# Turning the gated output of six head groups by a transposing transfer instead of TensorE transposes

## The chip, the cores and the metric

One core of one Trainium2 chip runs the whole program once. The metric is the device time of that run in microseconds (us); the median of three runs is what counts. Five engines work side by side, each on its own queue, in the order in which that queue was written: TensorE (PE) for products, VectorE (DVE), ScalarE (ACT) and GpSimd (POOL) for element work, and SyncE (SP), which here only starts transfers between memory and SBUF.

## The reference

The program is one decoder layer on 256 tokens of width 2048. A state-space part (SSD, 32 heads in 8 groups of 4) and an attention part (16 heads) read the same normalised input; their outputs, 2048 columns each, go together through `w_out`, and an MLP of width 8192 follows. What the change touches is the end of the SSD part:

```python
proj = jnp.einsum('bsd,de->bse', u, w_in)
z, xbc, dt_raw, q, k, v = jnp.split(proj, IN_SPLITS, axis=-1)
xbc = jax.nn.silu(causal_depthwise_conv(xbc, conv_w, conv_b))
...
y = ssd_chunked(xh, dt, a, bm, cm)
y = y + d_skip...[:, :, None] * xh
yg = y.reshape(b_, s_, SSM_GROUPS, -1) * jax.nn.silu(z.astype(f32)).reshape(b_, s_, SSM_GROUPS, -1)
yg = yg * lax.rsqrt(jnp.mean(yg * yg, axis=-1, keepdims=True) + EPS)
y_ssm = (yg.reshape(b_, s_, D_SSM) * ssm_norm_w.astype(f32)).astype(u.dtype)
...
return jnp.einsum('bse,ed->bsd', jnp.concatenate([y_ssm, y_att], axis=-1), w_out)
```

For each of the 8 groups the gated output `yg` is a block of 256 tokens by 256 columns in 32-bit numbers. It is computed with tokens on the partitions; the last product needs it with its columns on the partitions, so every block is turned (transposed) once.

## The kernel before, in words

**Products.** All large products run as three products of split numbers: ACT copies a 32-bit tile to a rounded `hi` (L150), DVE subtracts to get the rest `lo` (L151), and PE multiplies with both. Weights come in tiles of 256 rows by 512 columns (`raw`, four buffers, loaded by SP at L164, or by L159 and L160 where half of the tile was stored earlier). `hi` and `lo` have five buffers, so ACT and DVE can be at most five weight tiles ahead of PE. `gemm_features` gives columns on the partitions (16 products a tile, L540 and L543); `row_tile` gives tokens on the partitions (12 products, L382 to L384). Some tiles go through a scheme that saves one product in eight (`seven`, L469 to L471); it needs sums of weight tiles (L275, on DVE) and sums of the input (L428 to L431, on DVE, then split by L150 and L151), which go to buffers `tp`, `ah` and `al`.

**Order in time.** Up to 400 us the program computes B, C, a block of x, a unit for z and a second block of x, and then the same again for the other four groups (the second unit for z lies at 232 to 274 us); behind that come the blocks for q and k of the attention, and at 358 us a unit with token rows whose first `seven` is at 369 us. All that time PE works on these products; the SSD groups are side work in between.

**A group.** `ssd_group` is a generator that `pump` resumes: after each weight tile one waiting piece of work gets one turn. One group g loads its decay table `bc` (L859, ACT's queue; a tile of 128 x 1024 words, two buffers), makes `bn`, `xs`, `xdt` and others (L865 to L879), makes decay factors in place in `bc` (L895 and L896 on ACT, L897 on DVE, each for two chunks of 128 tokens), multiplies (PE L913, 8 small products that read `bc` and `xdt` and write a PSUM tile `ps`), adds and gates (DVE L916, L918), forms the sum of squares (ACT L922), its root (DVE L144, POOL L145) and scales (DVE L926, the last to write `yg`). Then PE turns `yg` by four transposes (L932) into a PSUM tile, and `split` writes it to `sh` and `sl` with the norm's weight (ACT L152, DVE L153). The PSUM tiles named `ps` (`psmall`) have two buffers.

**What sets the order.** The code gives the order in which work is offered; a scheduler then puts each instruction on its engine's queue by its own estimate of when it will be ready and by priorities. So an added wait can move instructions of other work on every queue. After the last group `drain` finishes the side work, the pool of the SSD tiles is closed (`ssd.close`), and its space goes to the buffers `ah`, `al`, `tp` of the next unit: their first loads and sums cannot start before the last reader of the SSD tiles is done.

Of the kernel before, what the change touches and what calls it, by code (L numbers as in the profile page):

```python
# [13 lines left out]
U16 = mybir.dt.uint16  # L14
AF = mybir.ActivationFunctionType
ALU = mybir.AluOpType

P = 128
S = 256
D = 2048  # L20
NT = S // P
# [23 lines left out]
AHEAD = 1_000_000  # L45
# [9 lines left out]
V_SEVENS = (1, 3, 5, 6)  # L55
QK_SEVENS = (1, 3, 5, 6)
PAIRS_AHEAD = 4
TURNS = ((1, 2, 4, 5), (3, 4, 8, 9))
LANDS = ((0, 3, 4, 6), (0, 6, 7, 10, 11))

# [20 lines left out]
def hymba_layer(ctx: ExitStack, tc: tile.TileContext, x, norm_mix_pre, w_in, conv_w, conv_b, dt_bias, a_log,  # L81
                d_skip, ssm_norm_w, w_out, norm_mix_post, norm_mlp_pre, w_up, w_down, norm_mlp_post,
                consts, out):
    nc = tc.nc
# [27 lines left out]
    sh = big.tile([P, NK, S], F32R, name="sh")  # L112
    sl = big.tile([P, NK, S], F32R, name="sl")
# [11 lines left out]
    ident = cp.tile([P, P], F32, name="ident")  # L125
# [12 lines left out]
    def psmall():  # L138
        return psm.tile([P, NB], F32, name="ps")
# [7 lines left out]
    def split(hi, lo, src, scale=None):  # L147

        if scale is None:
            return (nc.scalar.activation(hi, src, AF.Copy),  # L150
                    nc.vector.tensor_tensor(lo, src, hi.bitcast(F32), op=ALU.subtract))  # L151
        return (nc.scalar.activation(hi, src, AF.Copy, scale=scale),  # L152
                nc.vector.scalar_tensor_tensor(lo, src, scale, hi.bitcast(F32), op0=ALU.mult, op1=ALU.subtract))  # L153
# [104 lines left out]
    line, newest = {}, {}  # L258
# [34 lines left out]
    def next_pair():  # L293

        if not pairs:
            return
        src, (ca, c), k = pairs.pop(0)
        cb = slice(c, c + NB)
        d = places[len(paired) % len(places)]
        if len(paired) < len(places):  # L300
            nc.gpsimd.dma_start(d[:, 0:1], room["pairs"])
        nc.gpsimd.dma_start(d, src[k * KB * P:(k * KB + 1) * P, cb])
        nc.gpsimd.dma_start(d, src[(k * KB + 1) * P:(k * KB + 2) * P, cb], accum_op=ALU.add)
        paired.append((src, ca, k, d))

    paired = []
    places = [dram.tile([P, NB], F32, name=f"pair{i}") for i in range(PAIRS_AHEAD + 1)]

# [25 lines left out]

    waiting = deque()

    def pump(n=1):
        for _ in range(n):
            if waiting:
                work = waiting.popleft()  # L340
                if next(work, work) is not work:
                    waiting.append(work)

    def drain():
        while waiting:
            pump()
# [3 lines left out]
    def pump_beside(exact=False):  # L350

        if not beside:
            return
        work = beside.popleft()
        room["exact"] = exact
        with tc.issue_after(newest["act"].ins):
            next(work)
        flying.append(work)
# [143 lines left out]
    def unit(src, n, order, last, acc, more, combine, lag=0, at_end=(None, None), first=True, ending=None,  # L502
# [5 lines left out]
        for i, (k, by_seven) in enumerate(order):  # L508
            if i in TURNS[len(order) > 7]:
                pump_beside(len(order) > 7)  # L510
# [67 lines left out]
    w_pre, w_mlp, w_ssm, cb = par[:, 0:16], par[:, 16:32], par[:, 32:48], par[:, 48:80]  # L578
# [6 lines left out]
    rows = xp.tile([64, P], F32, name="rows")  # L585
# [132 lines left out]
    def steps():  # L718
# [5 lines left out]
        with tc.high_priority(offset=AHEAD):  # L724
            for _ in range(PAIRS_AHEAD):
                next_pair()
# [128 lines left out]
    def ssd_group(sp, g, bT, cT, xT, z):  # L855

        hs = slice(HPG * g, HPG * (g + 1))
        bc = sp.tile([P, HPG, S], F32, name="bc")
        nc.scalar.dma_start(bc, acs_d[hs].partition_broadcast(P))  # L859
        yield  # L860

        p = psmall()
        for c in range(NT):
            cs = slice(c * P, (c + 1) * P)
            nc.tensor.matmul(p[:, cs], bT[:, cs], cT[:, cs], start=True, stop=True)  # L865
        nc.tensor.transpose(p[:, S:S + P], bT[:, 0:P], ident)
        cbm = sp.tile([P, NT, P], F32, name="cbm")
        nc.vector.tensor_tensor(cbm, p[:, :S].rearrange("p (c i) -> p c i", c=NT),
                                triu[:, None, :].to_broadcast([P, NT, P]), op=ALU.mult)
        bn = sp.tile([P, P], F32, name="bn")  # L870
        nc.scalar.activation(bn, p[:, S:S + P], AF.Copy)

        p = psmall().rearrange("p (c f) -> p c f", c=NT)
        for c in range(NT):
            for f in range(2):
                nc.tensor.transpose(p[:, c, f * P:(f + 1) * P], xT[:, f, c * P:(c + 1) * P], ident)
        xs = sp.tile([P, NT, HPG, HD], F32, name="xs")
        nc.scalar.activation(xs.rearrange("p c r d -> p c (r d)"), p, AF.Copy)
        xdt = sp.tile([P, NT, HPG, HD], F32, name="xdt")  # L879
        for c in range(NT):  # L880
            nc.vector.tensor_tensor(xdt[:, c], xs[:, c], dt[:, c, hs, None].to_broadcast([P, HPG, HD]), op=ALU.mult)
        xdd = sp.tile([P, HPG, HD], F32, name="xdd")
        nc.gpsimd.tensor_tensor(xdd, xdt[:, 0], toend[:, hs, None].to_broadcast([P, HPG, HD]), op=ALU.mult)
        for c in range(NT):
            nc.gpsimd.tensor_tensor(xs[:, c], xs[:, c], skip_b[:, hs, None].to_broadcast([P, HPG, HD]), op=ALU.mult)
        yield

        for c in range(NT):
            m = bc[:, :, c * P:(c + 1) * P]
            for r in range(HPG):  # L890
                h = HPG * g + r
                if g in (2, 3):
                    nc.vector.tensor_scalar(m[:, r], m[:, r], acs[:, c, h:h + 1], 0.0, op0=ALU.subtract, op1=ALU.min)
                else:
                    nc.scalar.activation(m[:, r], m[:, r], AF.Relu, scale=-1.0, bias=acs[:, c, h:h + 1])  # L895
            nc.scalar.activation(m, m, AF.Exp, scale=1.0 if g in (2, 3) else -1.0)  # L896
            nc.vector.tensor_tensor(m, m, cbm[:, c, None, :].to_broadcast([P, HPG, P]), op=ALU.mult)  # L897

        p = psmall()
        nc.tensor.matmul(p[:, :S], bn, xdd.rearrange("p r d -> p (r d)"), start=True, stop=True)  # L900
        st = sp.tile([P, HPG * HD], F32, name="st")
        nc.scalar.activation(st, p[:, :S], AF.Copy)
        yield
        nc.tensor.matmul(p[:, S:], cT[:, P:], st, start=True, stop=True)
        yo = sp.tile([P, HPG, HD], F32, name="yo")
        nc.vector.tensor_tensor(yo, p[:, S:].rearrange("p (r d) -> p r d", r=HPG),
                                eacs[:, hs, None].to_broadcast([P, HPG, HD]), op=ALU.mult)
        nc.gpsimd.tensor_tensor(xs[:, 1], xs[:, 1], yo, op=ALU.add)
        yield
        p = psmall().rearrange("p (c r d) -> p c r d", c=NT, r=HPG)  # L910
        for c in range(NT):
            for r in range(HPG):
                nc.tensor.matmul(p[:, c, r], bc[:, r, c * P:(c + 1) * P], xdt[:, c, r], start=True, stop=True)  # L913

        yg = sp.tile([P, NT, HPG * HD], F32, name="yg")
        nc.vector.tensor_tensor(yg, p.rearrange("p c r d -> p c (r d)"), xs.rearrange("p c r d -> p c (r d)"),  # L916
                                op=ALU.add)
        nc.vector.tensor_tensor(yg, yg, z, op=ALU.mult)  # L918
        gs = sp.tile([P, NT], F32, name="gs")
        for c in range(NT):  # L920
            junk = sp.tile([P, HPG * HD], BF16, name="gj")
            nc.scalar.activation(junk, yg[:, c], AF.Square, accum_out=gs[:, c:c + 1])  # L922
        gr = sp.tile([P, NT], F32, name="gr")
        rsqrt_mean(gr, gs, HPG * HD)
        for c in range(NT):
            nc.vector.tensor_scalar(yg[:, c], yg[:, c], gr[:, c:c + 1], None, op0=ALU.mult)  # L926
        yield
        yield
        p = psmall().rearrange("p (f s) -> p f s", f=2)
        for f in range(2):  # L930
            for c in range(NT):
                nc.tensor.transpose(p[:, f, c * P:(c + 1) * P], yg[:, c, f * P:(f + 1) * P], ident)  # L932
        with tc.high_priority(offset=200):
            for f in range(2):
                k = 2 * g + f
                split(sh[:, k], sl[:, k], p[:, f], w_ssm[:, k:k + 1])

    sp = ssd.enter_context(tc.tile_pool(name="sp", bufs=2, side="right", reuse_waits="tile"))
    zs = []
    for hb in range(2):  # L940
# [4 lines left out]
        for xb in (2 * hb, 2 * hb + 1):  # L945
# [3 lines left out]
            for j in range(2):  # L949
                g = 2 * xb + j  # L950
# [56 lines left out]
    def keys_too(hb, pumps=(1,)):  # L1007
        return queries(COL_Q + hb * NB, rbq, pumps), queries(COL_K + hb * NB, rbc, pumps)
# [75 lines left out]

    qk = [keys_too(0, (2, 1))]
    drain()
    ssd.close()
    bigr = ctx.enter_context(tc.tile_pool(name="bigr", bufs=1, side="right", reuse_waits="tile"))
    att[1] = [bigr.tile([P, NK // 2, S], F32R, name=name) for name in ("ah1", "al1")]
# [455 lines left out]
    for b in range(2):  # L1545
        r = hp.tile([P, 2, S], F32, name="r", bufs=4)
# [87 lines left out]
```

## Time and profile before

| what | value |
|---|---|
| median of three runs | 1443.69 us (1441.72 to 1447.8) |
| profiled execution, own time | 1444.83 us |
| its span, first to last instruction | 1442.9 us |
| granted TensorE clock | 0.998 |
| PE busy | 1432.2 us (99%), 6930 products |
| DVE busy | 1297.6 us (90%) |
| ACT busy | 1003.1 us (70%) |
| moved by transfers | 340.30 MB |

The profiled execution lies 1.1 us above the median; 1.9 us of it lie before the first and after the last instruction. Products overlap in PE, so a product's duration in the profile is longer than its share of time: the distance from one start to the next tells what it takes.

### The profile page before, as it was taken

How to read it: one execution, taken by the hardware profiler on the slowest of the kernel's cores; microseconds unless marked ns; L12 is line 12 of the kernel's file. 1: busy time of each engine (PE TensorE's matmuls, PEld its weight loads, DVE VectorE, ACT ScalarE, POOL GpSimd, SP SyncE). 2: the span in 40 equal slices, each digit the busy share in tenths (PEclk: the TensorE clock that was granted, in tenths of full speed). 3: DMA queues.
4: the chain of work that ended last, by engine and by line, in shares of the span. 5: the costliest groups of instructions: out<-in, count | busy, mean ns of one | idle time of the engine just before them, and what ended most of it. 6: DMA issues, size and time to landing. Idle time of an engine off the chain costs nothing.

```text
span 1442.9 us, 20235 instructions
## 1 busy us (share of the span) xinstructions
PE 1432.2 (99%) x6930; PEld 1204.6 (83%) x6930; DVE 1297.6 (90%) x1881; ACT 1003.1 (70%) x1407; POOL 162.8 (11%) x244
## 2 busy tenths in 40 slices
PE   9999999999999999999999999999999999999998
PEld 8888888888888888888888888888888888887886
DVE  7788888988999778689988999999889999999998
ACT  7577669666666666656667669978565799978664
POOL 0301110121111000011100011010111011111000
PEclk9999999999999999999999999999999999999999
DMA  8977656756888648588976799799888899998954
GB/s 266 282 211 227 188 171 184 246 176 193 220 244 259 198 119 253 176 259 261 274 230 218 203 340 291 206 253 254 256 251 272 253 266 298 247 274 251 323 194 146
DMA packets 201926, 340.30 MB, mean 236 GB/s; under 512 B 45616, under 2 KB 48544, under 8 KB 201824
## 3 DMA queue, kind: packets, MB, share of 16 engines
q1 hardware_dynamic: 174304, 279.72, 61.7%
q0 software_dynamic: 19648, 45.63, 15.5%
q10 hardware_dynamic: 7872, 13.68, 2.9%
q8 instruction: 54, 0.88, 0.2%
q14 instruction: 48, 0.39, 0.1%
HBM read 327.39 MB, written 49.84 MB: 261 GB/s over the span
## 4 chain that ended last, share of the span: by engine, by line
PE 64%; DVE 5%; ACT 4%; DMA 2%; issue 2%; SPq 0%; ACTq 0%; DVEq 0%
PE acc L383 9%; PE acc L384 9%; PE acc L382 9%; PE acc L470 5%; PE acc L471 5%; PE acc L469 5%; PE acc L540 4%; PE ps L383 2%; PE ps L384 2%; PE ps L382 2%; PE acc L543 2%; ACT hi L150 2%; DVE lo L151 2%; PE ps L469 2%; PE ps L470 2%
## 5 line engine op out<-in xcount | busy, mean ns | idle before, releaser
L151 DVE TENSOR_TENSOR lo<-raw,hi 128x1024 fp32r<-128x1024 f32 (+1 forms) x390 | 473.2, 1218 | 79.0 <-ACT hi L150 77.2
L150 ACT ACTIVATE hi<-raw 128x1024 fp32r<-128x1024 f32 (+1 forms) x390 | 406.5, 1048 | 174.1 <-PE acc L384 51.2
L540 PE MATMUL acc<-ua,hi 128*128 128x512 f32 x520 | 141.2, 400 | 0.0
L150 ACT ACTIVATE hi<-e 128x1024 fp32r<-128x1024 f32 x66 | 69.9, 1059 | 53.6 <-DVE e L275 49.9
L540 PEld LDWEIGHTS acc<-ua,hi 128*128 128x128 f32 x520 | 91.3, 189 | 14.0
L382 PE MATMUL acc<-hi,ua 128*128 128x512 f32 x228 | 90.0, 395 | 0.0
L383 PE MATMUL acc<-lo,ua 128*128 128x512 f32 x228 | 89.2, 391 | 0.0
L384 PE MATMUL acc<-hi,ua 128*128 128x512 f32 x228 | 89.0, 390 | 0.0
L382 PE MATMUL acc<-hi,sh 128*128 128x512 f32 x220 | 86.7, 394 | 0.0
L383 PE MATMUL acc<-lo,sh 128*128 128x512 f32 x220 | 85.7, 390 | 0.0
L384 PE MATMUL acc<-hi,sl 128*128 128x512 f32 x220 | 85.7, 389 | 0.0
L543 PEld LDWEIGHTS acc<-ua,lo 128*128 128x128 f32 x520 | 76.5, 189 | 8.9
L151 DVE TENSOR_TENSOR lo<-e,hi 128x1024 fp32r<-128x1024 f32 x66 | 80.4, 1218 | 0.9 <-ACT hi L150 0.7
L543 PE MATMUL acc<-ua,lo 128*128 128x256 f32 x520 | 78.8, 281 | 0.0
L470 PE MATMUL acc<-lo,ah 128*128 128x512 f32 x180 | 70.1, 390 | 0.0
L471 PE MATMUL acc<-hi,al 128*128 128x512 f32 x180 | 70.0, 389 | 0.0
L469 PE MATMUL acc<-hi,ah 128*128 128x512 f32 x180 | 70.0, 389 | 0.0
L151 DVE TENSOR_TENSOR lo<-ha,hi 128x1024 fp32r<-128x1024 f32 x48 | 58.3, 1219 | 3.7 <-ACT hi L150 3.5
L540 PE MATMUL acc<-uc,hi 128*128 128x512 f32 x208 | 61.4, 405 | 0.0
L150 ACT ACTIVATE hi<-ha 128x1024 fp32r<-128x1024 f32 x48 | 50.3, 1050 | 9.4 <-PE acc L384 5.7
L469 PE MATMUL acc<-hi,ua 128*128 128x512 f32 x137 | 53.5, 390 | 0.0
L471 PE MATMUL acc<-hi,ua 128*128 128x512 f32 x137 | 53.3, 389 | 0.0
(578 smaller groups left out, 3724.7 us busy)
## 6 DMA issues: line engine op xcount, KB each, us to landing
raw<-in_w_in_dram SPq DMA_DIRECT2D x154, 512.0 KB, 4.4
raw<-in_w_down_dram SPq DMA_DIRECT2D x70, 512.0 KB, 5.7
raw<-in_w_up_dram SPq DMA_DIRECT2D x65, 512.0 KB, 4.8
raw<-in_w_out_dram SPq DMA_DIRECT2D x38, 512.0 KB, 5.3
raw<-pair SPq DMA_DIRECT2D x59, 256.0 KB, 4.5
pair<-in_w_up_dram POOLq DMA_DIRECT2D x56, 256.0 KB, 6.4
pair<-in_w_down_dram POOLq DMA_DIRECT2D x52, 256.0 KB, 6.0
ha<-in_w_up_dram SPq DMA_DIRECT2D x25, 512.0 KB, 6.0
```

The costliest lines, as they stand in the source:

```text
L150: return (nc.scalar.activation(hi, src, AF.Copy), nc.vector.tensor_tensor(lo, src, hi.bitcast(F32), op=ALU.subtract))
L151: nc.vector.tensor_tensor(lo, src, hi.bitcast(F32), op=ALU.subtract))
L382: nc.tensor.matmul(dst[:, cs], a_h[:, r, ts], hi[:, j, cs], start=begin and j == 0, stop=False)
L383: nc.tensor.matmul(dst[:, cs], a_h[:, r, ts], lo[:, j, cs], start=False, stop=False)
L384: product[t] = nc.tensor.matmul(dst[:, cs], a_l[:, r, ts], hi[:, j, cs], start=False, stop=end and j == KB - 1)
L469: nc.tensor.matmul(dst, a_h, hi[:, j], start=own and first, stop=False)
L470: nc.tensor.matmul(dst, a_h, lo[:, j], start=False, stop=False)
L471: nc.tensor.matmul(dst, a_l, hi[:, j], start=False, stop=own and last)
L540: nc.tensor.matmul(acc[f], hi[:, j, f * P:(f + 1) * P], u(k0 + j), start=k0 + j == 0, stop=False, skip_group_check=True)
L543: nc.tensor.matmul(acc[f][:, 0], lo[:, j, f * P:(f + 1) * P], u(k0 + j)[:, 0], start=False, stop=k0 + j == NK - 1, skip_group_check=True)
```

## The change

For groups 0 to 5 (`BY_PE = 6`) the block is not turned by PE. After the scaling (now L940), ACT copies `yg` into the first half of the group's own `bc` tile so that the low and the high 16-bit halves of the words lie apart (L956). SP issues one transposing transfer of 16-bit values from there back to `yg` (L957). The rest of the group's work, `normed_group`, is parked for 12 calls of `pump`; then ACT puts the halves together into the second half of `bc` (L962), and `split` (now L153 on ACT and L154 on DVE) reads `bc` in place of PSUM. Groups 6 and 7 keep the transposes (now L947). So 24 of 32 PE transposes go; 12 ACT copies of 128 x 1024 halves and six transfers on SP's queue come. `bc` is in use until the parked work is done, and it still has two buffers.

```diff
+BY_PE = 6
...
+    def park(work, calls):
+        parked.append([work, calls])
+
+    def land_parked(calls):
+        for one in parked:
+            one[1] -= calls
+        while parked and parked[0][1] <= 0:
+            with tc.issue_after(newest["act"].ins):
+                next(parked.popleft()[0], None)
+
     def pump(n=1):
+        land_parked(1)
...
         yield
+        if g >= BY_PE:
+            yield
+            p = psmall().rearrange("p (f s) -> p f s", f=2)
...
+            return
+        halves, whole = (bc.rearrange("p (i r) s -> p i (r s)", i=2)[:, i] for i in range(2))
+        words = yg.rearrange("p c n -> p (c n)").bitcast(U16)
+        with tc.issue_after(newest["act"].ins):
+            nc.scalar.activation(halves.bitcast(U16).rearrange("p (h n) -> p h n", h=2), words.rearrange("p (n h) -> p h n", h=2), AF.Copy)
+        nc.sync.dma_start_transpose(words.rearrange("p (n s) -> p n s", s=P), halves.bitcast(U16))
+        park(normed_group(g, words, whole), 12)
+
+    def normed_group(g, words, whole):
+
+        nc.scalar.activation(whole.bitcast(U16).rearrange("p (n h) -> p h n", h=2), words.rearrange("p (h n) -> p h n", h=2), AF.Copy)
+        rows = whole.rearrange("p (c f s) -> p f c s", c=NT, f=2)
+        for f in range(2):
+            k = 2 * g + f
+            split(*(v[:, k].rearrange("p (c s) -> p c s", c=NT) for v in (sh, sl)), rows[:, f], w_ssm[:, k:k + 1])
...
     drain()
+    land_parked(AHEAD)
     ssd.close()
```

The lines of the unchanged code move by 14 behind it in `ssd_group` (L913 is L927, L916 is L930, L897 is L911), by 1 in `split` and the loads, by 14 in `row_tile` (L382 is L396), `seven` (L469 is L483) and `products` (L540 is L554, L543 is L557).

The scheduler moves work by it. On PE, before, the small products of groups 6 and 7 (L913) and their transposes (L932) stand between whole weight tiles of the block for k (`ua`, `ub`, `uc` are the input, by parts):

```order
L913 MATMUL ps<-xdt,bc 128x64 x8
L540 MATMUL acc<-ua,hi 128x512 x8
L543 MATMUL acc<-ua,lo 128x256 x8
L913 MATMUL ps<-xdt,bc 128x64 x8
L540 MATMUL acc<-ua,hi 128x512 x8
L543 MATMUL acc<-ua,lo 128x256 x8
L540 MATMUL acc<-ua,hi 128x512 x8
L543 MATMUL acc<-ua,lo 128x256 x8
L932 MATMUL ps<-ident,yg 128x128 x8
L540 MATMUL acc<-ub,hi 128x512 x8
L543 MATMUL acc<-ub,lo 128x256 x8
```

After, the products of group 6 (L927) stand in the last two tiles of that block:

```order
L557 MATMUL acc<-ub,lo 128x256 x8
L554 MATMUL acc<-uc,hi 128x512
L927 MATMUL ps<-xdt,bc 128x64 x4
L554 MATMUL acc<-uc,hi 128x512 x7
L557 MATMUL acc<-uc,lo 128x256 x8
L927 MATMUL ps<-xdt,bc 128x64 x4
L554 MATMUL acc<-uc,hi 128x512 x2
```

Behind the rest of that tile come 17 products of the next unit, and then, still on PE, this:

```order
L927 MATMUL ps<-xdt,bc 128x64 x4
L947 MATMUL ps<-ident,yg 128x128 x4
L398 MATMUL acc<-hi,ua 128x512
L396 MATMUL acc<-hi,ua 128x512
L927 MATMUL ps<-xdt,bc 128x64 x4
L397 MATMUL acc<-lo,ua 128x512
L398 MATMUL acc<-hi,ua 128x512
L396 MATMUL acc<-hi,ua 128x512
L397 MATMUL acc<-lo,ua 128x512
L398 MATMUL acc<-hi,ua 128x512
L947 MATMUL ps<-ident,yg 128x128
L396 MATMUL ps<-hi,ua 128x512
```

The products of group 7 and the transposes of both groups have moved from the block for k into the unit behind it, five products apart; that unit's `acc` products stand ahead of them, and its 24 `ps` products, the last ahead of the first `seven`, behind.

On ACT, the loads of `bc` for groups 6 and 7 (L873) stand after the change behind the copies that put groups 4 and 5 together (L962), where before they stood close together and earlier, among work on the block for x:

```order
L962 ACTIVATE bc<-yg 128x2x512
L153 ACTIVATE sh<-bc,par 128x256 x2
L151 ACTIVATE hi<-raw 128x1024
L873 DMA bc<-acs_d 128x1024
L962 ACTIVATE bc<-yg 128x2x512
L151 ACTIVATE hi<-raw 128x1024
L909 ACTIVATE bc<-bc,acs 128x128 x4
L151 ACTIVATE hi<-raw 128x1024
L910 ACT_TABLE_LOAD
L910 ACTIVATE bc<-bc 128x4x128
```

Group 6's decay factors (L909) now stand close behind its own load; group 7's load follows only behind group 5's `split`.

More of the change, by code (lines that the diff above doesn't have):

```diff
@@ L335, in hymba_layer @@
     waiting = deque()
+    parked = deque()
+    def park(work, calls):
[6 more added lines that the diff above has]
+                next(parked.popleft()[0], None)
     def pump(n=1):
+        land_parked(1)
         for _ in range(n):
@@ L927, in ssd_group @@
         yield
-        yield
[L929 to L936, printed above, removed]
+        if g >= BY_PE:
+            yield
+            p = psmall().rearrange("p (f s) -> p f s", f=2)
+            for f in range(2):
+                for c in range(NT):
+                    nc.tensor.transpose(p[:, f, c * P:(c + 1) * P], yg[:, c, f * P:(f + 1) * P], ident)
+            with tc.high_priority(offset=200):
+                for f in range(2):
+                    k = 2 * g + f
+                    split(sh[:, k], sl[:, k], p[:, f], w_ssm[:, k:k + 1])
+            return
[8 more added lines that the diff above has]
+        rows = whole.rearrange("p (c f s) -> p f c s", c=NT, f=2)
+        for f in range(2):
+            k = 2 * g + f
+            split(*(v[:, k].rearrange("p (c s) -> p c s", c=NT) for v in (sh, sl)), rows[:, f], w_ssm[:, k:k + 1])
+        yield
     sp = ssd.enter_context(tc.tile_pool(name="sp", bufs=2, side="right", reuse_waits="tile"))
```

## The prediction

> **What bounds the kernel now.** I read the page's shares first, then the chain that ended last, then PE's waits.
>
> ```profile
> PE 1432.2 (99%) x6930; PEld 1204.6 (83%) x6930; DVE 1297.6 (90%) x1881; ACT 1003.1 (70%) x1407; POOL 162.8 (11%) x244
> PE 64%; DVE 5%; ACT 4%; DMA 2%; issue 2%; SPq 0%; ACTq 0%; DVEq 0%
> ```
>
> PE is busy for 1432.2 of 1442.9 us, so two things move the end: work taken off PE, and time in which PE stands still. The waits of PE say how much it stands still today:
>
> ```profile
> PE ps L382 <- ACT hi L150: 1.5, 1, 1.5
> PE ps L1463 <- ACT dg L1462: 1.4, 1, 1.4
> PE ps L591 <- DVE half L580: 1.1, 1, 1.1
> PE ps L383 <- DVE lo L151: 1.0, 2, 0.8
> ```
>
> Nothing there names the transposes (L932) or the products ahead of them (L913): the SSD side work is hidden completely. PE takes its queue in order, so that holds only while each of these instructions finds its data ready. DVE's 90% is an average; by stage (us of the window, then PE, PEld, DVE, ACT busy):
>
> ```profile
> 240.00:260.00 20.00, 20.00 (x90) 16.53 (x90) 18.93 (x31) 18.01 (x26) 2.13 (x5) 1.00 0.65 180
> 330.00:358.00 28.00, 28.00 (x175) 25.11 (x174) 22.45 (x39) 15.14 (x31) 3.42 (x5) 1.00 0.62 189
> 358.00:396.00 38.00, 38.00 (x171) 31.46 (x170) 37.51 (x54) 24.57 (x29) 5.48 (x8) 1.00 0.82 228
> ```
>
> From 358 us on DVE works 37.51 of 38 us beside a full PE. There DVE has no slack at all, and whatever delays its start there delays PE.
>
> **What is removed.** The 24 transposes of groups 0 to 5:
>
> ```profile
> L932 PE MATMUL ps<-ident,yg x32: 270/272/273, 182.8 to 349.8; 128*128 128x128 f32 x32
> 182.80 0.60 PE L932 MATMUL ps<-ident,yg 128*128 128x128 f32 x4
> 183.15 2.07 PE L540 MATMUL acc<-ua,hi 128*128 128x512 f32 x8
> ```
>
> One is 272 ns long, but four start at 182.80 and the next product at 183.15: 0.35 us per group. Six groups give back 6 x 0.35 = 2.1 us. That is the gain, and it is all of it.
>
> The Trainium skill, "TensorE: Matmul & The Clock Gate", Part 4, puts a 128x128 transpose in a kernel's context at about 275 ns; the row's 272 ns agrees as a duration, the starts do not. By its figure the gain would be an estimated 24 x 0.275 = 6.6 us. "VectorE: DVE Perf Modes", in its rules for kernel authors, says to transpose on TensorE if a PSUM destination is acceptable and by the DMA crossbar otherwise, which speaks against this change: the destination here was PSUM.
>
> **What is added off PE.** The MLP of this program has the same copies and transfers:
>
> ```profile
> L1515 ACT ACTIVATE mw<-hb x4: 1059/1210/1364, 947.2 to 970.3; 128x1024 uint16<-128x1024 uint16 x4
> L1525 SPq DMA_TRANSPOSE hb<-ha x8: 1237/1252/6033, 1142.3 to 1288.6; - x8
> DMA to landing us min/median/max: 2.7/6.1/11.7
> ```
>
> Twelve copies at 1.21 us are 14.5 us of ACT, spread over 200 us in which ACT has idle time (15.14 of 28 us at 330 to 358): 0 us on the path. A transfer holds SP's queue 1.2 us and lands after 6.1 us in the middle, 11.7 at most; the block for k takes two turns of `pump` and one in alternate weight tiles, so that twelve turns are eight tiles or more. A tile takes 2.80 us, by the starts below (352.76 to 355.56), so 8 x 2.80 = 22.4 us cover it: 0 us. Uncovered, each would cost up to 11.7 us.
>
> ```profile
> 352.76 2.00 PE L540 MATMUL acc<-uc,hi 128*128 128x512 f32 x8
> 354.60 1.11 PE L543 MATMUL acc<-uc,lo 128*128 128x256 f32 x8
> 355.56 0.63 PE L540 MATMUL acc<-uc,hi 128*128 128x512 f32 x2
> 358.34 0.40 PE L382 MATMUL acc<-hi,ua 128*128 128x512 f32 x1
> 358.57 0.40 PE L383 MATMUL acc<-lo,ua 128*128 128x512 f32 x1
> ```
>
> (The last two give 0.23 us for a row product.)
>
> **What is moved.** The parked work holds `bc`. With two buffers, group g+2 can load its decay table only when group g is put together. Groups 2 and 3 behind 0 and 1: their products are spread over four tiles; the order leaves room for most of the load, I take 0.5 us (0 to 3.5). Groups 2 and 3 now end in the unit for z, in which DVE gets four more L154; at 0.474 us each (row below) these are 1.9 us beside 18.93 of 20: I take 1.0 (0 to 1.9). The last groups matter most. These rows carry them:
>
> ```profile
> L859 ACTq DMA_DIRECT2D bc<-acs_d x8: 326/326/415, 92.4 to 306.2; - x8
> DMA to landing us min/median/max: 3.8/5.2/5.7
> L895 ACT ACTIVATE bc<-bc,acs x48: 382/388/425, 103.7 to 331.9; 128x128 f32<-128x128 f32 x48
> L896 ACT ACTIVATE bc<-bc x16: 612/632/647, 106.6 to 332.4; 128x512 f32<-128x512 f32 x16
> L897 DVE TENSOR_TENSOR bc<-bc,cbm x16: 675/936/1103, 136.9 to 333.2; 128x512 f32<-128x512 f32 x16
> L153 DVE SCALAR_TENSOR_TENSOR sl<-ps,par,sh x16: 470/474/480, 186.3 to 355.5; 128x256 fp32r<-128x256 f32 x16
> L916 DVE TENSOR_TENSOR yg<-ps,xs x8: 673/683/692, 158.5 to 343.7; 128x512 f32<-128x512 f32 x8
> L918 DVE TENSOR_TENSOR yg<-yg,tk x8: 674/684/692, 163.4 to 344.9; 128x512 f32<-128x512 f32 x8
> ```
>
> *Group 6's table.* Its load waits for group 4's split; landing, factors and L911 then run beside four to five feature tiles. Nearly covered: 0.5 us (0 to 2.1).
>
> *Group 7's table.* Its load waits for DVE's last L154 of group 5, which stands behind group 6's L930, which waits for group 6's second set of L927. From there: L930 0.68, L154 0.48, load 5.2, five L909 at 0.388 1.9, exp 0.63, L911 0.94 (the old L895 to L897), together 9.8 us. On PE stand one tile (2.80) and 17 row products (3.9) in between, 6.7 us. PE waits 3.1 us (1.5 with a landing of 3.8 and L911 at 0.68, 3.8 with 5.7 and 1.10).
>
> *Group 7's own chain.* Between its last L927 and its first transpose (L947) PE has five row products, 1.1 us. The chain between them has these pieces:
>
> ```profile
> 346.50 0.40 ACT L922 ACTIVATE gj<-yg 128x256 bf16<-128x256 f32 x1
> 346.81 0.19 ACT L922 ACTIVATION_READ_ACCUMULATOR gj<-yg 128x1 f32 x1
> 347.77 0.16 DVE L144 TENSOR_SCALAR rm<-gs 128x2 f32<-128x2 f32 x1
> 348.01 0.69 POOL L145 TENSOR_TENSOR gr<-rm,half 128x2 f32<-128x2 f32 x1 [3.83 <-DVE rm L144]
> 348.74 0.62 DVE L926 TENSOR_SCALAR yg<-yg,gr 128x256 f32<-128x256 f32 x2 [0.81 <-POOL gr L145]
> 349.08 1.03 PE L932 MATMUL ps<-ident,yg 128*128 128x128 f32 x8
> ```
>
> L930 0.68, one L154 of group 6 0.48, L932 0.68, two L936 at 0.59 1.18, DVE 0.16, POOL 0.69, half of L940 0.31: 4.2 us and some 0.3 for the hand-overs. PE waits 4.5 - 1.1 = 3.4 us (3.0 to 3.7). This one has no scatter in it but a row's own, and alone it eats the gain.
>
> *The unit behind.* The first sum and the loads of the `seven` scheme use the SSD tiles' space and start when the last transpose is through. Before:
>
> ```profile
> 350.27 0.37 SPq L164 DMA_DIRECT2D ah<-in_w_in_dram  x1
> 350.57 0.68 DVE L428 TENSOR_TENSOR tp<-ua 128x512 f32<-128x512 f32 x1
> 368.12 1.22 DVE L151 TENSOR_TENSOR lo<-tp,hi 128x1024 fp32r<-128x1024 f32 x1
> 369.25 0.39 PE L469 MATMUL acc<-hi,ua 128*128 128x512 f32 x1
> 370.84 0.39 PE L470 MATMUL acc<-lo,ah 128*128 128x512 f32 x1
> ```
>
> From the first sum (350.57) to the end of the `lo` that the first `seven` needs (369.34) DVE worked 18.8 us, and PE had 20 us of other products (to 370.84). After, PE has 24 `ps` products and six of the `seven` left behind the transposes, 30 x 0.227 = 6.8 us. DVE has fewer rows there than before: two `lo` of weight tiles (2 x 1.15 by starts), four L564, two L1004 and one L153 have gone ahead, about 5.6 us, so 13.1 us are left. PE waits 13.1 - 6.8 = 6.3 us. From below: with loads alone the last tile of `tp` lands about 8 us after the release, then sum, `hi` and `lo`, 10.9 in all, 4.1 us of wait; from above all of the old work, 12 us. It is not won back: behind it DVE is as full as PE.
>
> **The sum.** -2.1 + 0.5 + 1.0 + 0.5 + 3.1 + 3.4 + 6.3 = +12.7 us. On the profiled execution's 1444.8 us (1442.9 and 1.9 around it) that is 1457.5; the median lies 1.1 us below it, so 1456 us for the median. All lower ends together give +6.5 (1450), all upper ends +25 (1468).
>
> **Rivals.** A measurement of this kernel tells a change above about 0.5%, 7.2 us, from none.
>
> *Everything stays hidden: 1442 us.* PE gives back 2.1 us, and the order puts L927 and L947 where PE's data are ready on the chip as in the scheduler's estimate. For it: today's waits name no SSD line. Against: group 7's chain cannot run in 1.1 us. It decides if the chip shows that chain's end ahead of PE.
>
> *Only the queue's waits cost, the unit behind does not: 1450 us.* 12.7 - 6.3 = +6.4. For it: while PE waits, DVE can run ahead; against: the sums need the released space, and no wait before brings that earlier.
>
> *The transfers come late: 1470 and more.* Then L962 holds ACT's queue, the `hi` of later tiles behind it, and so PE. It decides from about 14 us (five buffers of 2.80 us) on; four of six transfers late by the 3.7 us between 11.7 and, say, 8 would add 15. Against: 22.4 us of parking.
>
> *The transposes cost their durations: 1452 us.* 24 x 0.272 = 6.5 us gained instead of 2.1. Against: the starts above. This is what the skill's figure would make of it.
>
> **Chances.** My forecast 0.56; queue's waits alone 0.17; hidden 0.12; transfers late 0.07; durations 0.04; something that gains more than 7 us 0.04, for which I see no row. The range is 1443 to 1468: it leaves out half of the hidden case, the gain and the late transfers, 0.17. Slower by over 0.5% (above 1450.9) is the forecast, the late transfers, the durations and a third of the queue's waits, 0.73; same is the rest of the queue's waits and the hidden case, 0.23; faster 0.04.
>
> **What would show it.** In the new profile PE's waits should name L927 or L947 on ACT, DVE or the load, 1 to 3.5 us each, and L484 or L483 on DVE's `lo`, some 6 us, all between 340 and 390 us; `bc`'s last load should start after 350 us instead of at 306; group 7's L947 should start near 366 us (17 row products, 3.9, and the waits of 0.5, 3.1 and 3.4 behind 355.6) instead of 349. From 400 us on everything should be shifted by one amount. It is wrong if the first `seven` starts as early as before (369 us, less 2), if PE's waits keep their sum, or if `bc`'s last loads land well ahead of L909.

## The result, and the profile after

The changed kernel takes 1466.49 us (median of five runs, 1463.0 to 1469.49) against 1444.37 us (five runs, 1441.72 to 1447.97): ratio 1.0148, interval 1.0127 to 1.0169, or 22 us slower. The profiled execution's span is 1466.5 us against 1442.9. The forecast was 1456: the direction was right, the size some 10 us short.

The page after, shares of the span and of the chain that ended last:

```profile
PE 1439.2 (98%) x6906; PEld 1204.8 (82%) x6906; DVE 1299.8 (89%) x1881; ACT 1015.1 (69%) x1417; POOL 163.3 (11%) x244
PE 82%; DVE 7%; DMA 4%; ACT 4%; issue 2%; POOL 0%; SPq 0%; ACTq 0%; DVEq 0%
```

PE has 24 instructions fewer and is busy 7 us longer. ACT's 12 us more are the 12 copies (6 x 1.06 and 6 x 1.37 = 14.5 us by their rows at the end); its share was 70% and is 69%. PE's waits after (who waited for whom: us in total, times, longest):

```profile
PE acc L483 <- ACT hi L151: 4.9, 2, 4.3
PE ps L947 <- DVE yg L940: 2.9, 1, 2.9
PE ps L879 <- ACT bn L885: 2.6, 2, 1.6
PE ps L927 <- DVE bc L911: 2.5, 2, 1.7
PE ps L397 <- DVE lo L152: 1.4, 3, 0.8
PE ps L927 <- issue: 1.3, 1, 1.3
PE acc L554 <- DVE cT L578: 1.2, 1, 1.2
PE acc L554 <- ACT hi L151: 1.0, 1, 1.0
```

Before, no wait named L913 or L932; now L927 (old L913), L947 (old L932) and the first `seven` (L483) stand at the top. The whole list adds up to 22.5 us against 6.0 us before, 16.5 us more.

The tail in order of time (start, duration; in brackets the idle time before it and what ended it):

```profile
353.22 1.14 PE L927 MATMUL ps<-xdt,bc 128*128 128x64 f32 x8 [1.72 <-DVE bc L911]
364.47 1.57 ACT L909 ACTIVATE bc<-bc,acs 128x128 f32<-128x128 f32 x5 [1.45 <-DMA bc<-acs_d]
366.60 0.69 DVE L911 TENSOR_TENSOR bc<-bc,cbm 128x512 f32<-128x512 f32 x1 [0.95 <-ACT bc L910]
367.39 1.07 PE L927 MATMUL ps<-xdt,bc 128*128 128x64 f32 x8 [1.32 <-issue]
370.26 0.69 DVE L930 TENSOR_TENSOR yg<-ps,xs 128x512 f32<-128x512 f32 x1 [0.32 <-PE ps L927]
373.88 0.62 DVE L940 TENSOR_SCALAR yg<-yg,gr 128x256 f32<-128x256 f32 x2 [0.80 <-POOL gr L146]
374.38 0.30 PE L947 MATMUL ps<-ident,yg 128*128 128x128 f32 x1 [2.95 <-DVE yg L940]
374.42 0.68 DVE L442 TENSOR_TENSOR tp<-ua 128x512 f32<-128x512 f32 x1
375.83 0.38 SPq L165 DMA_DIRECT2D ah<-in_w_in_dram  x1
388.76 1.22 DVE L152 TENSOR_TENSOR lo<-tp,hi 128x1024 fp32r<-128x1024 f32 x1
389.62 0.80 PE L483 MATMUL acc<-hi,ua 128*128 128x512 f32 x1 [4.32 <-ACT hi L151]
```

This is the chain the prediction wrote down: group 6's products wait for the factors, ACT waits for group 7's table, group 7's transposes wait for the scaling, and only then (375.83; before at 350.27) does the first load go into the space of the SSD tiles. The wait at 367.39, put down to "issue", ends when the factors of the row above are done (366.60 + 0.69).

One loss stands in no list of waits. Windows after (the seventh column, behind the five engines, is the granted clock of PE):

```profile
348.00:358.00 10.00, 8.29 (x42) 6.96 (x42) 4.32 (x5) 7.69 (x15) 0.27 (x1) 0.83 0.56 174
372.00:380.00 8.00, 5.62 (x20) 4.56 (x21) 4.89 (x12) 2.70 (x8) 0.69 (x1) 0.79 0.38 115
390.00:396.00 6.00, 6.00 (x17) 4.56 (x17) 5.97 (x8) 2.52 (x3) 0.62 (x1) 0.57 0.82 189
```

And two of its products in order of time (start, duration):

```profile
376.34 0.63 PE L396 MATMUL ps<-hi,ua 128*128 128x512 f32 x1
376.77 0.63 PE L397 MATMUL ps<-lo,ua 128*128 128x512 f32 x1
```

Behind the waits products start 0.43 us apart (376.34, 376.77) instead of 0.23, in three stretches: 354 to 358, 374 to 378, 389 to 395 us. By the starts they cost 1.5, 1.7 and 2.7 us, 5.9 in all. (A fourth stretch, near 1335 us, is there before as well, near 1312 us.) So 16.5 of waits + 5.9 of slow products - 2.1 gained = 20.3 of the 23.6 us between the two spans; 3 us of the profiled pair are not assigned.

Where the time arises can be read from one group of products, before and after (first and last start):

```profile
L469 PE MATMUL acc<-hi,uc x22: 389/389/389, 389.0 to 1258.9; 128*128 128x512 f32 x22
L483 PE MATMUL acc<-hi,uc x22: 389/389/389, 409.8 to 1281.3; 128*128 128x512 f32 x22
```

The first starts 20.8 us later, the last 22.4. The other 2.8 of the 23.6 us come behind the changed part, in code that the change does not touch; 0.9 us of the waits lie there.

### The profile page after: what moved, and what is told of

The parts are those of the page before. It is cut to its first block, busy times and chain, and to the rows that moved or that the text cites. A ratio compares the mean times of both kernels' runs of the same rounds, so it can differ in the third digit from the quotient of the medians.

```text
span 1466.5 us, 20199 instructions
## 1 busy us (share of the span) xinstructions
PE 1439.2 (98%) x6906; PEld 1204.8 (82%) x6906; DVE 1299.8 (89%) x1881; ACT 1015.1 (69%) x1417; POOL 163.3 (11%) x244
## 4 chain that ended last, share of the span: by engine, by line
PE 82%; DVE 7%; DMA 4%; ACT 4%; issue 2%; POOL 0%; SPq 0%; ACTq 0%; DVEq 0%
PE acc L554 11%; PE acc L396 10%; PE acc L397 10%; PE acc L398 10%; PE acc L484 6%; PE acc L485 6%; PE acc L483 6%; PE acc L557 5%; DVE lo L152 3%; PE ps L397 2%; PE ps L398 2%; PE ps L396 2%; PE ps L484 2%; PE ps L485 2%; PE ps L483 2%
## 5 line engine op out<-in xcount | busy, mean ns | idle before, releaser
L151 ACT ACTIVATE hi<-raw 128x1024 fp32r<-128x1024 f32 (+1 forms) x390 | 406.0, 1048 | 177.8 <-PE acc L398 53.3
L554 PE MATMUL acc<-ua,hi 128*128 128x512 f32 x520 | 141.6, 400 | 2.1 <-DVE cT L578 1.2
L151 ACT ACTIVATE hi<-e 128x1024 fp32r<-128x1024 f32 x66 | 69.9, 1059 | 53.5 <-DVE e L276 48.1
L554 PEld LDWEIGHTS acc<-ua,hi 128*128 128x128 f32 x520 | 91.4, 189 | 16.6 <-DVE cT L578 1.4
L396 PE MATMUL acc<-hi,ua 128*128 128x512 f32 x228 | 89.7, 396 | 0.0
L397 PE MATMUL acc<-lo,ua 128*128 128x512 f32 x228 | 89.6, 393 | 0.0
L398 PE MATMUL acc<-hi,ua 128*128 128x512 f32 x228 | 89.2, 391 | 0.0
L396 PE MATMUL acc<-hi,sh 128*128 128x512 f32 x220 | 86.5, 393 | 0.0
L557 PEld LDWEIGHTS acc<-ua,lo 128*128 128x128 f32 x520 | 76.6, 189 | 8.9
L557 PE MATMUL acc<-ua,lo 128*128 128x256 f32 x520 | 79.3, 282 | 0.0
L483 PE MATMUL acc<-hi,ah 128*128 128x512 f32 x180 | 70.0, 391 | 0.5 <-ACT hi L151 0.5
L554 PE MATMUL acc<-uc,hi 128*128 128x512 f32 x208 | 62.8, 413 | 0.0
L483 PE MATMUL acc<-hi,ua 128*128 128x512 f32 x137 | 53.7, 393 | 4.3 <-ACT hi L151 4.3
L151 ACT ACTIVATE hi<-ha 128x1024 fp32r<-128x1024 f32 x48 | 50.2, 1050 | 9.7 <-PE acc L398 4.5
L484 PE MATMUL acc<-lo,ua 128*128 128x512 f32 x137 | 53.7, 392 | 0.0
```

Source lines behind the costliest of these rows:

```text
L151: return (nc.scalar.activation(hi, src, AF.Copy), nc.vector.tensor_tensor(lo, src, hi.bitcast(F32), op=ALU.subtract))
L396: nc.tensor.matmul(dst[:, cs], a_h[:, r, ts], hi[:, j, cs], start=begin and j == 0, stop=False)
L397: nc.tensor.matmul(dst[:, cs], a_h[:, r, ts], lo[:, j, cs], start=False, stop=False)
L398: product[t] = nc.tensor.matmul(dst[:, cs], a_l[:, r, ts], hi[:, j, cs], start=False, stop=end and j == KB - 1)
L483: nc.tensor.matmul(dst, a_h, hi[:, j], start=own and first, stop=False)
L484: nc.tensor.matmul(dst, a_h, lo[:, j], start=False, stop=False)
```

## The experiments

Two theories at first. **Hold**: the parked work keeps the decay table `bc` occupied, so that the loads of the last groups, and all that follows them, come late. **Work**: the copies, the transfers and the splits from SBUF cost by themselves, about 22.1 / 6 = 3.7 us for each group.

**1. Only the buffer held, nothing turned by transfer.**

```diff
-        if g >= BY_PE:
+        if True:
...
+            if g < BY_PE:
+                park(held_on(bc), 12)
             return
+    def held_on(bc):
+        nc.scalar.activation(bc[:, 0, 0:1], bc[:, 0, 0:1], AF.Copy)
+        yield
```

> All eight groups are turned by TensorE as before; only, for groups 0 to 5, `bc` is kept occupied for 12 turns of `pump` by a copy of one column of it onto itself. No transfer, no halves, no split from SBUF. Hold theory (the time comes from the decay table's buffer staying occupied, which moves the last groups' loads and products back and lets PE wait): most of the change's 22 us stays, 1455 to 1467, with PE waits at L927 or L947 between 350 and 380 us and a late first `seven`. Work theory (the copies, the transfers and the split from SBUF cost by themselves): 1444 plus or minus 3.

Measured: 1462.08 us, ratio 1.0126 (1.0111 to 1.0141), 18 us slower. Its waits of PE, and then the row of its loads of `bc` (durations in ns, first and last start):

```profile
PE acc L483 <- ACT hi L151: 5.8, 2, 4.3
PE ps L947 <- DVE yg L940: 2.4, 3, 1.2
PE ps L879 <- ACT bn L885: 1.4, 1, 1.4
PE ps L927 <- DVE bc L911: 1.0, 1, 1.0
PE ps L927 <- issue: 0.9, 1, 0.9
```

```profile
L873 ACTq DMA_DIRECT2D bc<-acs_d x8: 326/327/445, 92.2 to 345.4; - x8
```

No group is turned by a transfer in it, there is no copy of halves and no split from SBUF in the groups, and some four fifths of the loss are there, at the same instructions. The last load starts at 345.4 us (306.2 before, 359.4 after). The work theory has fallen as the main cause.

**2. Which groups.**

```diff
-BY_PE = 6
+BY_PE = 4
```

> Only groups 0 to 3 are turned by transfer; groups 4 to 7 as before. Hold theory: the tail is as before, left are the waits at 205 us (2.3), at 280 to 290 us (some 2.5) and the 1.4 gained: 1447, between 1444 and 1451. Work theory, 22.1 / 6 = 3.7 us for each turned group: 1444.4 + 4 x 3.7 = 1459.

Measured: 1446.1 us, ratio 1.0027 (1.0009 to 1.0045).

```diff
-        if g >= BY_PE:
+        if g not in (4, 5):
```

> Only groups 4 and 5 are turned by transfer. Hold theory: the whole tail stays, by the stalls of the changed kernel after 340 us 17.5 us, less 0.7 gained: 1461 (1457 to 1465). Work theory, 3.7 us for each turned group: 1444.4 + 2 x 3.7 = 1452.

Measured: 1461.32 us, ratio 1.0117 (1.01 to 1.0134). PE's waits with only groups 4 and 5:

```profile
PE acc L483 <- ACT hi L151: 4.3, 1, 4.3
PE ps L947 <- DVE yg L940: 2.9, 1, 2.9
PE ps L927 <- DVE bc L911: 2.1, 1, 2.1
PE ps L927 <- issue: 1.5, 1, 1.5
```

Two groups give 17 us, four give 4 us (the ratios above of 1444): it is not a price per group. Groups 4 and 5 hold the buffers that groups 6 and 7 need, and behind group 7 comes the release.

**3. Shorter parking.**

```diff
-        park(normed_group(g, words, whole), 12)
+        park(normed_group(g, words, whole), 4)
```

> As the change, parked for 4 turns of `pump` instead of 12. Hold theory: `bc` is free eight turns earlier, the products and transposes of groups 6 and 7 stand in the block for k again, and most of the tail's loss goes: 1447 (1443 to 1453). Work theory: the same work, 1466. A third case, that the transfers need the long parking: their 3.9 us in the middle against 4 turns (2 or more weight tiles, 5.6 us or more) let ACT wait, 1466 or more.

Measured: 1453.04 us, ratio 1.0066 (1.0051 to 1.0081). More than half of the loss goes, less than I expected (1447, at most 1453).

The same with 1 in place of 4:

> As the change, but parked for one turn of `pump` only. Hold theory: `bc` is free after the copies and the transfer alone (1.06 + 3.9 + 1.37 us and the splits): 1449 (1444 to 1453), not more than the 1453 of 4 turns. If transfers then come too late for ACT, PE waits for `hi` behind L962 and the time is above 1453.

Measured: 1454.55 us, ratio 1.0067 (1.0047 to 1.0087), no better than four turns and above the expected 1444 to 1453. Here a second price shows. ACT's row in this run:

```profile
183.97 1.34 ACT L962 ACTIVATE bc<-yg 128x1024 uint16<-128x1024 uint16 x1 [4.45 <-DMA yg<-bc]
```

ACT's queue reaches the put-together before the transfer has landed and stands for 4.45 us; PE then waits 4.9 us, until 187.6 us (for `bn`, which ACT makes behind it), and from 187.5 to 193 us its granted clock is 0.50. Parking too long holds the buffer, parking too short holds ACT.

**4. Nothing held: halves elsewhere.** `xs` and the group's part of `z` are dead when `yg` is gated. The halves go to `xs`, the put-together words to `z`.

```diff
-        halves, whole = (bc.rearrange("p (i r) s -> p i (r s)", i=2)[:, i] for i in range(2))
+        halves = xs.rearrange("p c r d -> p (c r d)")
...
-        park(normed_group(g, words, whole), 12)
+        park(normed_group(g, words, z), 12)
...
-        nc.scalar.activation(whole.bitcast(U16).rearrange("p (n h) -> p h n", h=2), ...
-        rows = whole.rearrange("p (c f s) -> p f c s", c=NT, f=2)
+        nc.scalar.activation(whole.bitcast(U16).rearrange("p c (n h) -> p h c n", h=2), words.rearrange("p (h c n) -> p h c n", h=2, c=NT), AF.Copy)
+        rows = whole.rearrange("p c (f s) -> p f c s", f=2)
```

> As the change, all six groups by transfer and parked for 12 turns, but the halves are laid in the group's `xs` and put together in its part of the gate `z`, both dead by then, so that `bc` is free as early as before; its eight loads stand on ACT's queue where they stood before. Hold theory: the tail's waits and the slow products behind them go, the 2.1 us of TensorE are gained: 1443 (1440 to 1448; the upper end if the last put-together of groups 4 and 5 holds the release of the SSD tiles). Work theory: the same copies, transfers and splits, 1466.

Measured: 1449.66 us, ratio 1.0035 (1.0022 to 1.0048). Its row of the loads, and then two of its waits of PE:

```profile
L873 ACTq DMA_DIRECT2D bc<-acs_d x8: 326/326/417, 92.1 to 303.8; - x8
```

```profile
PE ps L947 <- DVE yg L940: 1.5, 2, 0.8
PE ps L914 <- POOL xdd L897: 1.4, 2, 1.0
```

All six groups are turned by transfer, with the same copies and splits, and some 16 of the 22 us are gone. The loads are where they were (303.8), the first `seven` does not wait, and between 350 and 400 us no product is slow (granted clock 1.00). What is left, 5 us, was not expected: 1449.66 lies above the 1443 and above its upper bound, 1448.

Then only groups 0 to 3 in this way (`BY_PE = 4`):

> As the run with the halves in `xs` and `z`, but only groups 0 to 3 by transfer; groups 4 to 7 as before. Hold theory: 1.4 us gained and nothing lost, 1442 to 1444, the first version that could be faster than the kernel before, by less than these rounds can tell. Work theory: 1459.

Measured: 1441.58 us, ratio 0.9984 (0.9973 to 0.9995). And the same kernel a second time:

> The run of groups 0 to 3 by transfer with the halves in `xs` and `z`, again with five rounds: 0.998 of the kernel before, 1441.6, if the 2 us below it are real (1.4 us are accounted for by the 16 transposes that are gone); 1.000 if they were scatter.

Measured: 1442.41 us, ratio 0.9990 (0.9980 to 1.0001). In both batches the median is 1 to 2 us below the kernel before, which is about the 1.4 us that the prediction's term gives; the second interval just reaches 1. It is the only version that was not slower than before, and that its whole time is shorter is likely, not shown. The traces show the gain itself. The product of section "The result" that started at 389.0 us before starts here, in the two runs, at

```profile
L483 PE MATMUL acc<-hi,uc x22: 389/389/389, 386.4 to 1258.1; 128*128 128x512 f32 x22
L483 PE MATMUL acc<-hi,uc x22: 388/390/390, 386.9 to 1260.4; 128*128 128x512 f32 x22
```

which is 2.6 and 2.1 us earlier. With all six groups it starts at 389.6, 3.2 us behind the first of these, and PE's waits at L947 (1.5) and L914 (1.4), shown above, make up most of that.

The 5 us of all six groups were tried once more with four turns of parking:

> All six groups by transfer with the halves in `xs` and `z`, parked for 4 turns. With 12 turns this took 1449.7, where groups 4 and 5 are put together between 340 and 350 us. If what is left there comes from this late end (DVE's splits of groups 4 and 5 among the chain of groups 6 and 7), four turns bring 1443 (1441 to 1446); if it comes from `xs` being held until the transfer lands (POOL's L897 1.4 us late in that run), it stays at 1448 to 1451.

Measured: 1447.46 us, ratio 1.0024 (1.0012 to 1.0036): between the two cases. Why groups 4 and 5 still make PE wait there stays open, and so does the part of the 5 us that arises behind 390 us.

**5. The slow products.** In the changed kernel 14 products without use were put ahead of group 7's transposes, where PE stands still.

```diff
+            if g == 7:
+                h_, l_, r = act_u(0)
+                for _ in range(14):
+                    nc.tensor.matmul(p.rearrange("p (k s) -> p k s", k=2), h_[:, r, 0:P], h_[:, r:r + 2], start=True, stop=True)
```

> As the change, with 14 products of 128x512 (3.2 us at 0.227), whose result nobody uses, on TensorE ahead of the four transposes of group 7, where PE stood for 3.1 us. If the slow products behind that wait (0.43 instead of 0.227 us each from 374 to 378 us, 1.7 us in all) come from the standing still, the clock granted there stays at 1.0 and the time falls by 1.5 us, to 1465; the trace tells this better than the time. If they come from something else at that place, PE is as slow behind the 14 products as before and the time is 1466 to 1467.

Measured: 1463.29 us, ratio 1.0127 (1.0105 to 1.0149). The time fell by 3 us where 1.5 were expected, but its interval overlaps the changed kernel's; the trace decides. The window from 374 to 378 us, of the changed kernel and of this run:

```profile
374.00:378.00 4.00, 3.62 (x11) 2.95 (x12) 2.80 (x8) 0.95 (x2) 0.00 (x0) 0.58 0.27 42
```

```profile
374.00:378.00 4.00, 4.00 (x21) 3.07 (x20) 3.23 (x9) 1.20 (x3) 0.12 (x1) 1.00 0.35 63
```

The 14 products in this run's order of time:

```profile
371.31 3.43 PE L948 MATMUL ps<-ua 128*128 128x512 f32 x14
```

The granted clock goes from 0.58 to 1.00, and 21 products instead of 11 run in these 4 us. The slow products of this stretch come from PE's standing still; for the other two stretches that is inferred from the same picture.

It gave back almost no time, though. The first `seven` still waits for `hi`:

```profile
389.35 0.79 PE L483 MATMUL acc<-hi,ua 128*128 128x512 f32 x1 [4.30 <-ACT hi L151]
```

It starts at 389.35 instead of 389.62, and its waits come to 5.6 us instead of 4.9: PE was through its products sooner and waited longer. So the 3 us between the two medians are not explained by this stretch.

**6. The release alone.** The kernel before, with a chain of small POOL operations on `yg` behind group 7's transposes: only the release of that tile moves.

```diff
+        if g == 7:
+            for _ in range(16):
+                nc.gpsimd.tensor_tensor(yg[:, 0, 0:2], yg[:, 0, 0:2], half[:, :2], op=ALU.mult)
```

> The kernel before, with 16 small operations on POOL, one behind the other, on two columns of group 7's `yg` behind its transposes (0.70 us each by L145), so that the release of that tile comes at 350.1 + 11.2 = 361.3 us instead of 350.1 and nothing else is added to TensorE, ACT or DVE. By the release step of the prediction: the loads into `ah` start 11 us later and their last landing moves from 356.9 to 368; DVE's L275, which stands in its queue ahead of other sums, starts 9.2 us later, less some 2 us of slack: PE waits some 7 us ahead of the first products of the `seven`, 1451 (1446, if only the loads' own chain counted, to 1453). Rival (the wait there came from DVE's sums standing behind group 7's own chain, not from the release): 1444.

Measured: 1448.18 us, ratio 1.0032 (1.002 to 1.0045). With 28:

> The same with 28 operations: release at 369.7, landing at 376.4, L275 17.6 us later, PE waits 15.6 us (9.8 if only the loads' own chain counted), and if a long wait lowers the clock behind it, 1 to 3 us more: 1461 (1454 to 1463). One us of release costs one us of time between the two runs. Rival: 1444.

Measured: 1450.89 us, ratio 1.0047 (1.003 to 1.0064). The start of the first load into the space and PE's wait, with 16 operations:

```profile
358.33 0.37 SPq L164 DMA_DIRECT2D ah<-in_w_in_dram  x1
```

```profile
PE acc L470 <- DVE lo L151: 2.8, 1, 2.8
```

and with 28:

```profile
361.35 0.37 SPq L164 DMA_DIRECT2D ah<-in_w_in_dram  x1
```

```profile
PE acc L470 <- DVE lo L151: 5.6, 1, 5.6
```

The POOL operations took less than I had put in (8.40 us for the 16 and 11.18 us for the 28), so the release moved by 8.1 and 11.1 us only, and the expectations were too high; the second lies below its bounds. The step itself holds: 3.0 us of release made 2.8 us of wait, at the place named, and the slack before it counts is 8.1 - 2.8 = 5.3 us.

The two runs also differ behind the wait. Here are the stretch around the wait of the run with 16 (granted clock 1.00), and two products behind the wait of the run with 28:

```profile
350.00:400.00 50.00, 47.05 (x216) 38.00 (x215) 45.49 (x68) 28.86 (x38) 13.21 (x25) 1.00 0.76 226
```

```profile
377.45 0.63 PE L471 MATMUL acc<-hi,al 128*128 128x512 f32 x1
377.88 0.63 PE L469 MATMUL acc<-hi,ah 128*128 128x512 f32 x1
```

Behind 5.6 us of wait the products started 0.43 us apart until 382.6 us, which cost 2.6 us more; behind 2.8 us of wait they did not.

## Why the prediction was right or wrong

- **The cause and the place**: right. The held buffer, the late loads, the chain of group 7 and the late release are what the runs show; experiments 1 and 4 take the cause by itself, and without it. The waits at the places named came to 12.8 us where the sum had 14.8. That they are so close is in part luck: single terms, below, were wrong by up to 1.8 us, to both sides.
- **The gain**: read a little too small. 0.35 us per group was the term, from the start of the four transposes (182.80) to that of the next product (183.15). But the eight products behind them took 1.91 us (183.15 to 185.06) where eight take 1.84 (352.76 to 354.60), so that a group costs 0.42 us, 2.5 for six:

```profile
185.06 0.64 PE L543 MATMUL acc<-ua,lo 128*128 128x256 f32 x4
```

The two batches of experiment 4 with 16 transposes fewer lie 1.2 to 2.2 us below before by the medians, and 2.1 and 2.6 by the traces at 389 us; 4 x 0.42 is 1.7. The durations, 16 x 0.272 = 4.4 us, are outside both intervals (0.9973 of 1443.8 is 3.9 us).
- **Copies and transfers at nothing**: right for groups 0 to 3 (experiment 4), with the condition that the transfer has landed (park of one turn). It landed after 3.1 to 4.9 us in the changed kernel, faster than the 6.1 us of the MLP's that I had used. With groups 4 and 5 as well, some 5 us are left that neither this nor the hold explains.
- **Group 7's own chain**: 3.4 predicted, 2.9 measured.
- **Group 7's table**: 3.1 predicted, 1.3 measured.
- **Group 6's table**: 0.5 predicted, 1.7 measured.
- **The unit behind**: 6.3 predicted, 4.9 measured at the waits. From the first sum (374.42) to the end of the `lo` (388.76 + 1.22) 15.6 us passed instead of my 13.1; PE's cover was longer too, as 34 products stood in it, not 30, and some of them were slow. The prediction also said that DVE has no slack from 358 us on; in experiment 6 the release could come 5.3 us later before PE waited.
- **Groups 2 and 3, and the unit for z**: 0.5 and 1.0 predicted. The waits for L578 (1.2) and at one L927 (0.8), from 206 to 208 us, belong to groups 2 and 3, 1.9 us; in the unit for z (232 to 274 us) PE stands still for less than 0.1 us.
- **From 281 to 325 us**: nothing predicted. PE waits for `hi` (L554, 1.0) and for `bn` (L879, 2.6, less 0.6 that its old line L865 had), 3.0 us. The run that only holds the buffer has such waits too (L879, 1.4, and L890, 1.2), and with the halves elsewhere L879 is back at 0.6, so the waits for `bn` belong to the hold.
- **The step that failed** is the sum, which priced each wait at its own length: "PE waits" 3.4 and 6.3 us with products at 0.227 us behind them. A term is missing from it. The products behind the waits started 0.43 us apart (granted clock 0.58 in the window from 374 to 378 us) and cost 5.9 us more, over half of the 10 us that the forecast was short. Of these, most of the 1.7 us from 374 to 378 us would have been waited at the first `seven` instead (experiment 5). Also missing are the 3.0 us from 281 to 325 us and the 2.8 us behind 400 us; 2.0 us too much stood in the waits named.

  The Trainium skill, "TensorE: Matmul & The Clock Gate", in its section "Why this matters for your kernels", asks for no idle gaps of PE above some 3 us; I had cited that page for the transposes alone. The trace does not agree on the length: the waits ahead of the slow stretches were 1.72, 2.95 and 4.32 us, two of them shorter. It agrees on the slow spacing (0.43 us; the page's Part 1 has 426.7 ns for 512 columns when cold).
- **The signs named beforehand**: L927 and L947 at 1 to 3 us and the first `seven` on its weights are there; the last load at 359.4 is "after 350"; group 7's transposes came at 374.4, not 366; the first `seven` waits for `hi` (L151) where I had named `lo`. From 400 us on the shift is not one amount: 20.8 us at first, 23.6 at the end.

## What to carry to other kernels

When work is taken off the bounding engine and parked, ask first what it holds meanwhile: a buffer kept 12 turns longer cost some 18 us here, the work itself little. A place that is already dead (`xs`, `z`) removes the wait without any new space. And where the bounding engine runs at full clock, a wait can cost more than its length, because the products behind it can run slow as well (here behind waits of 1.72, 2.95 and 4.32 us). It costs that only where no other wait follows that would have been longer by as much.

## What the runs showed of the hardware

- **The clock falls after short waits.** A PE wait of 2.95 us (374.38) was followed at once by products 0.43 us apart for about 3.5 us; with the wait filled the clock stayed at 1.00. It did not happen every time: two waits of 1.2 and 0.8 us close together (206 to 208 us) were followed by none, and so was the 2.8 us of the run with 16 POOL operations; behind the 1.72 us at 353.22 it happened. A length from which it happens can't be read from these runs.
- **Small transposes on TensorE cost less than their duration.** Each is 272 ns long, but four of them cost PE about 0.42 us; what decides is the distance between starts, that of the products behind them included.
- **The two 16-bit copies differ**: taking apart took 1.06 us, putting together 1.37 us, for the same 128 x 1024 halves:

```profile
L956 ACT ACTIVATE bc<-yg x6: 1041/1057/1059, 167.6 to 323.0; 128x1024 uint16<-128x1024 uint16 x6
L962 ACT ACTIVATE bc<-yg x6: 1357/1365/1384, 192.7 to 343.4; 128x1024 uint16<-128x1024 uint16 x6
```
